# A third pair of k tiles by seven products, and a feed-forward in smaller parts with its down projection between the units

## The chip, the cores and the metric

The kernel runs on one core of one Trainium2 chip. The metric is the time of one execution on the device in microseconds (us), as the median of several runs. The engines of the core work side by side, each through its own list of instructions in order: TensorE (PE) multiplies matrices into PSUM banks, VectorE (DVE) and ScalarE (ACT) do elementwise work, GpSimd (POOL) a little more of that, and SyncE (SP) issues the transfers from memory.

## The reference

The reference is an encoder trunk of two residual layers over 256 tokens of width 2048, all in float32. Layer 0 mixes tokens by grouped-query attention, layer 1 by a gated recurrent block. After either mixer comes the same feed-forward, with its own weights, and that is where the change lies:

```python
def rms_norm(x, g):
    xf = x.astype(jnp.float32)
    y = xf * lax.rsqrt(jnp.mean(xf * xf, axis=-1, keepdims=True) + EPS)
    return (y * g.astype(jnp.float32)).astype(x.dtype)

def swiglu(h, w_gate, w_up, w_down):
    return (jax.nn.silu(h @ w_gate) * (h @ w_up)) @ w_down

# every layer i:
#   x = x + mixer(rms_norm(x, norm_mix[i]))
#   x = x + swiglu(rms_norm(x, norm_ffn[i]), ffn_w_gate[i], ffn_w_up[i], ffn_w_down[i])
```

`w_gate` and `w_up` are 2048 x 5632, `w_down` is 5632 x 2048.

## The kernel before

**Precision.** Every float32 operand is split into a high part (`hi`) and a low part (`lo`), and a product is three matmuls: high x high, low x high, high x low (`product`, lines 253 to 259; L255, L256 and L258 are those three). For weights, a transfer of 512 KB fills a buffer `raw` (128 x 1024), ScalarE casts it to `hi` (L110) and VectorE subtracts to get `lo` (L111). `raw`, `hi` and `lo` have five buffers each, so weights are made a few transfers ahead of their use and no further.

**One feed-forward unit.** The 5632 hidden columns are worked in 11 units of 512 columns (`unit` in `ffn`, lines 670 to 703). The 16 k tiles of the normed activations are taken as 8 pairs `c`. A pair in the plain way takes one transfer of `w_gate` and one of `w_up`, and each meets two k tiles, two halves of the tokens and three matmuls: 24 matmuls of 128x512 per pair. A pair named in `SEVEN` is worked by a 2x2 block scheme with seven products in place of eight (Strassen's in Winograd's form; the blocks are token halves by k tiles on one side and k tiles by gate and up on the other): 21 matmuls. `load_seven` (lines 115 to 139) makes what it needs of the weights: one wide cast (L123) and subtraction (L124), four additions of 128x512 (L126) for the sums `ws`, a narrow cast (L127) and subtraction (L128), and two wide casts (L131) and subtractions (L132) for the high and low parts `wsh`, `wsl` of the sums. The sums have one buffer each. The activations' side of the scheme (`form`, lines 382 to 395) is made once per layer and pair when the norm's input is turned, column group by column group.

The accumulators are PSUM banks of two pools of four. `m1, p5, p7, p6` are taken from one (`bank`, tag `pm`), `c11, c21, c12, c22` from the other (`new_acc`, tag `acc`). When the last pair in `SEVEN` is over, ScalarE copies `m1` (L688) and VectorE combines the first four banks (L689 to L692). At the unit's end VectorE adds `c11` and `c21` (L695), ScalarE applies Silu, VectorE makes the gated product (L698, L699) and turns it in 32x32 blocks (L339), ScalarE sets the blocks in place in sixteen copies (L346), and the result is split into an `act` tile (L701, L702).

**The down projection** runs over four groups of 512 output columns (`wide_project`, two banks each, 12 matmuls per transfer), and each group is added to the residual `x_tm` (`add_residual`, L279).

**Order.** The hidden columns are cut in parts of 16, 16 and 12 tiles of 128, four, four and three units. The kernel runs the units of the first part; then for each part the first unit of the next one, the whole down projection of this part, and the other units of the next. So units follow each other in rows of five, four and two. The last part's down projection (`groups`) runs its first two column groups over all but the last unit's tiles first. TensorE's order is that of the program text. The order on the other engines is set by the framework's planner, which simulates all engines with its own cost figures and sends instructions out as they become ready; on the chip each engine then keeps that order. The order of the weight transfers is written out beforehand (`ffn_order`) and must agree with the program's.

Of the kernel before, what the change touches and what calls it, by code (L numbers as in the profile page):

```python
# [13 lines left out]
F32R = mybir.dt.float32r  # L14
# [4 lines left out]
P = 128  # L19
S = 256  # L20
# [4 lines left out]
GROUP = NQ // NKV  # L25
NBLK = 8
DFF = 5632
PARTS = [16, 16, 12]
UNIT = 4
SEVEN = (0, 4)  # L30
HALF = 8
CHUNK = HALF * P
WIDE = 512
NW = D // WIDE
# [33 lines left out]
def trunk(ctx, tc, w, out):  # L68
    nc = tc.nc
    act, dve, pool, pe, sync = nc.scalar, nc.vector, nc.gpsimd, nc.tensor, nc.sync  # L70
# [3 lines left out]
    xp = ctx.enter_context(tc.tile_pool(name="xp", bufs=16))  # L74
# [7 lines left out]
    def nm(s):  # L82
        uid[0] += 1
        return f"{s}_{uid[0]}"

    def tmp(tag, shape=(P, S), dt=F32, bufs=2):
        pl = tp if tag in COMMON else scope[-1]
        return pl.tile(list(shape), dt, tag=tag, name=nm(tag), bufs=bufs)
# [50 lines left out]
    def halves(src):  # L139
        return [src[:, a : a + HALF, :] for a in range(0, KT, HALF)]  # L140

    def pairs(src):
        return [src[c] for c in range(src.shape[0])]

    def out_order(src, late=1):
        groups = [pairs(src[g]) for g in range(NW)]
        return sum([g[:-late] for g in groups[:2]] + [g[-late:] for g in groups[:2]] + groups[2:], [])

    def ffn_order(l):
        at = np.cumsum([0] + PARTS) // UNIT  # L150
        units = []
        for i in range(at[-1]):
            both = [(w[f"w_gate{l}"][i, c], w[f"w_up{l}"][i, c]) for c in range(KT // 2)]
            units.append(sum(([b] if c in SEVEN else list(b) for c, b in enumerate(both)), []))
        seq = sum(units[: at[1]], [])
        for p in range(len(PARTS)):
            more = units[at[p + 1] : at[p + 2]] if p + 1 < len(PARTS) else []
            down = w[f"w_down{l}_{p}"]
            seq += sum(more[:1], []) + (sum(map(pairs, down), []) if more else out_order(down, UNIT // 2)) + sum(more[1:], [])
        return seq  # L160

    order = [w["w_k"][i] for i in range(2 * KT // 4)]
    order += sum((halves(w["w_qv"][h % 20]) for h in range(NQ, NQ + 20)), [])
# [1 line left out]
    for b in range(-1, NBLK):  # L165
        xin = range(2 * b + 2, 2 * b + 4) if b + 1 < NBLK else []
        yin = range(KT + 2 * b, KT + 2 * b + 2) if b >= 0 else []
        both = [halves(w["w_in"][c]) for c in (*xin, *yin)]
# [4 lines left out]
    def half():  # L173
        n = taken[0]
        taken[0] += 1
        if n == 0:
            return load_half(order[n], 2, partial(load_x, 0, 4))
        if n < KT // 2 and n % 2 == 0:
            load_x(2 * n, 4)
        if n == KT // 2 - 2:  # L180
            load_tables()
        got = (load_seven if isinstance(order[n], tuple) else load_half)(order[n])
        if n == KT // 2 + 1:
            follow(sync.dma_start(out=x_tm, in_=w["xt"]), newest["load"])
        if n in (KT // 2 + 2, KT // 2 + 3):
            token_squares(n - KT // 2 - 2)
        return got
# [22 lines left out]
    def new_acc():  # L210
        return ps_a.tile([P, 2 * S], F32, tag="acc", name=nm("acc"))
# [49 lines left out]
    def wide(accs, xs, k0, total, fresh=None):  # L261
        hi, lo = half()
        fresh = fresh or (k0 == 0, k0 == 0)
        for j in range(CHUNK // WIDE):
            k = k0 + j
            wh, wl = (t[:, j * WIDE : (j + 1) * WIDE] for t in (hi, lo))
            for a in range(2):
                product(accs[a], block(xs, k, a), (wh, wl), j == 0 and fresh[a], k == total - 1)

    def wide_project(xs, total):  # L270
        accs = [new_acc() for _ in range(2)]
        for k0 in range(0, total, 2):
            wide(accs, xs, k0, total)
        return accs

    def add_residual(g, accs, norm, store=False):
        for a in range(2):
            o = x_tm[:, a, g * WIDE : (g + 1) * WIDE]
            dve.tensor_tensor(o, o, accs[a], ALU.add)  # L279
            if store:  # L280
                sync.dma_start(out=out[:, a, g * WIDE : (g + 1) * WIDE], in_=o)
        if norm is not None:
            norm.add(g)

    def groups(xs, total, ready, between, done):
        front = [[new_acc() for _ in range(2)] for _ in range(2)]
        for accs in front:
            for k0 in range(0, ready, 2):
                wide(accs, xs, k0, total)
        between()  # L290
        for g in range(NW):
            for k0 in range(ready, total, 2) if g < 2 else ():
                wide(front[g], xs, k0, total)
            done(g, front[g] if g < 2 else wide_project(xs, total))
# [23 lines left out]
    at = ctx.enter_context(ExitStack())  # L318
# [30 lines left out]
    class Norm:  # L349
# [24 lines left out]
        def turn(self, g):  # L374
# [3 lines left out]
            for i in range(2):  # L378
                if self.g[0] == "norm_ffn" and 2 * g + i in SEVEN:
                    self.form(2 * g + i, t[:, 2 * i : 2 * i + 2, :])  # L380

        def form(self, c, src):
# [4 lines left out]
            for i, x, y, op in (  # L387
# [3 lines left out]
                pool.tensor_tensor(t[:, i, :], x, y, op)  # L391
            hi, lo = (tmp(f"f{n}", (P, 4, P), F32R, bufs=len(SEVEN)) for n in "hl")
            act.copy(hi, t)
# [222 lines left out]
        later(d_sc, scores)  # L616

    def act_four():
        return xp.tile([P, UNIT, 2 * S], F32R, tag="act", name=nm("act"), bufs=5)

    def act_tiles(n):
        return [t[:, i, :] for t in [act_four() for _ in range(n // UNIT)] for i in range(UNIT)]
# [43 lines left out]
    def ffn(norm, nxt):  # L666
        def bank():
            return ps_m.tile([P, 2 * S], F32, tag="pm", name=nm("pm"))

        def unit():  # L670
            xs, r = norm.xs, [norm.r[:, a : a + 1] for a in range(2)]
            m1, p5, p7, p6 = (bank() for _ in range(4))
            c11, c21, c12, c22 = (new_acc() for _ in range(4))
            for c in range(KT // 2):
                if c not in SEVEN:
                    wide((c11, c21), xs, 2 * c, KT, (False, False))
                    wide((c12, c22), xs, 2 * c, KT, (False, c == 1))
                    continue
                wt, first, end = half(), c == SEVEN[0], c == SEVEN[-1]
                n1, n3, n2, n4 = norm.forms[c]  # L680
                a11, a12, a22 = block(xs, 2 * c, 0), block(xs, 2 * c + 1, 0), block(xs, 2 * c + 1, 1)
                for o, x, y in ((m1, a11, "b11"), (p5, n1, "t1"), (p7, n3, "t3"), (p6, n2, "t2")):
                    product(o, x, wt[y], first, end)
                for o, x, y in ((c21, a22, "t4"), (c11, a12, "b21"), (c12, n4, "b22")):
                    product(o, x, wt[y], first, False)
                if end:
                    base, v, u, x = (tmp(f"e{i}", (P, 2 * S), bufs=1) for i in range(4))
                    act.copy(base, m1)  # L688
                    dve.tensor_tensor(u, base, p6, ALU.add)  # L689
                    dve.tensor_tensor(v, u, p5, ALU.subtract)  # L690
                    dve.tensor_tensor(u, u, p7, ALU.add)
                    dve.tensor_tensor(x, u, p5, ALU.subtract)  # L692
            h = tmp("hid", (P, 2, 2 * S), bufs=1)
            for o, y, b in ((base, base, c11), (u, u, c21)):
                dve.tensor_tensor(o, y, b, ALU.add)  # L695
            for a, (o, y, b) in enumerate(((base, v, c12), (u, x, c22))):
                table_act(o, o, AF.Silu, scale=r[a])
                dve.tensor_tensor(h[:, a, :], b, y, ALU.subtract)  # L698
                dve.scalar_tensor_tensor(h[:, a, :], h[:, a, :], r[a], o, ALU.mult, ALU.mult)  # L699
            t, ht = act_four(), turn_blocks(h, (act,), h)  # L700
            act.copy(t[:, :, :S], ht)  # L701
            dve.tensor_tensor(t[:, :, S:], ht, t[:, :, :S].bitcast(F32), ALU.subtract)  # L702
            return [t[:, k, :] for k in range(UNIT)]

        hid = sum((unit() for _ in range(PARTS[0] // UNIT)), [])
        for p in range(len(PARTS)):
            last = p == len(PARTS) - 1
            cur = hid
            hid = [] if last else unit()
            if last:  # L710
                groups(cur, PARTS[p], PARTS[p] - UNIT, lambda: None, partial(add_residual, norm=nxt, store=nxt is None))
            else:
                for g in range(NW):
                    add_residual(g, wide_project(cur, PARTS[p]), None)
                hid += sum((unit() for _ in range(PARTS[p + 1] // UNIT - 1)), [])
        if nxt is not None:
            nxt.finish()
        scope.pop()
        ft.pop().close()


    nr = Norm("norm_mix", KT)
    ffn(nf, nr)


# [101 lines left out]
    units = [(d, j) for j in range(2) for d in range(2)]  # L827
    blk = nxt = None
    for b in range(-1, NBLK):
        blk, nxt = nxt, Block(b + 1) if b + 1 < NBLK else None  # L830
# [102 lines left out]
```

## Time and profile before

| | |
|---|---|
| median of 3 runs | 2021.25 us (2019.75 to 2022.85) |
| the profiled execution | 2023.0 us, of which its span 2021.3 us |
| granted TensorE clock, mean of the span | 0.995 |
| TensorE busy | 1997.4 us, 99% |
| VectorE busy | 1516.7 us, 75% |
| ScalarE busy | 1290.8 us, 64% |
| GpSimd busy | 232.4 us, 11% |

All times of the trace are counted from the span's start. The first feed-forward begins at 279.3 us and ends about 982; the second begins about 1314 and ends with the span. A busy share is an average over stages, so what matters is read from windows cut at a stage's edges. In a row of a timeline stand start, duration, engine, line, operation, output and inputs, and in brackets how long the engine was idle before and what ended that. Matmuls overlap in the pipeline, so their spacing says more than their durations.

### The profile page before, as it was taken

The numbers are of one execution on the slowest core, as the hardware profiler recorded it, in microseconds if no ns is written. First come the engines' busy times: TensorE is split into PE (matmuls) and PEld (weight loads), VectorE is DVE, ScalarE is ACT, GpSimd is POOL, SyncE is SP. The second block draws the span as 40 slices with busy tenths as digits, with TensorE's granted clock in tenths as the row PEclk, the third lists the DMA queues.
The fourth block names the chain that finished last, engine by engine and source line by source line (L and its number), as shares of the span: only waits on it lengthen the run. The fifth ranks groups of instructions, "written<-read, shape, count | busy, mean of one in ns | idle before, by whom it ended". The sixth has DMA issues, their size and how long they took to land.

```text
span 2021.3 us, 27692 instructions
## 1 busy us (share of the span) xinstructions
PE 1997.4 (99%) x9994; PEld 1702.7 (84%) x9994; DVE 1516.7 (75%) x1958; ACT 1290.8 (64%) x1999; POOL 232.4 (11%) x317
## 2 busy tenths in 40 slices
PE   9999999999999999999899999999999999999999
PEld 7888888888888888888799998888888888888887
DVE  7888688886568865686678886888885578856764
ACT  7566576667446664467779996877665457654562
POOL 0464130000000000001333340400000000000000
PEclk9999999999999999999999999999999999999999
DMA  8444565655666656665555555665666655666654
GB/s 315 135 137 131 182 198 193 209 197 179 216 188 198 208 188 208 197 199 188 173 176 178 190 170 179 188 198 187 208 210 196 195 189 189 215 199 195 199 181 155
DMA packets 108569, 386.04 MB, mean 191 GB/s; under 512 B 12176, under 2 KB 12432, under 8 KB 108304
## 3 DMA queue, kind: packets, MB, share of 16 engines
q1 hardware_dynamic: 108288, 384.26, 58.8%
q8 instruction: 78, 1.28, 0.3%
q14 instruction: 59, 0.48, 0.1%
q10 hardware_dynamic: 144, 0.02, 0.0%
HBM read 382.13 MB, written 2.10 MB: 190 GB/s over the span
## 4 chain that ended last, share of the span: by engine, by line
PE 91%; DVE 3%; POOL 2%; issue 1%; DMA 1%; ACT 1%; SPq 0%; POOLq 0%; ACTq 0%; DVEq 0%
PE acc L258 24%; PE acc L256 24%; PE acc L255 24%; PE acc L235 3%; PE acc L236 3%; PE acc L237 3%; PE pm L258 2%; PE pm L256 2%; PE pm L255 2%; PE acc L224 1%; POOL hb L503 1%; DVE lo L111 1%; PE pm L237 1%; PE pm L236 1%; PE pm L235 1%
## 5 line engine op out<-in xcount | busy, mean ns | idle before, releaser
L111 DVE TENSOR_TENSOR lo<-raw,hi 128x1024 fp32r<-128x1024 f32 (+1 forms) x617 | 754.5, 1235 | 374.4 <-ACT hi L110 369.5
L110 ACT CAST hi<-raw 128x1024 fp32r<-128x1024 f32 (+1 forms) x617 | 639.5, 1049 | 538.2 <-PE acc L256 503.7
L255 PE MATMUL acc<-hi,xg 128*128 128x512 f32 x1100 | 428.0, 389 | 0.0
L256 PE MATMUL acc<-hi,xg 128*128 128x512 f32 x1100 | 428.0, 389 | 0.0
L258 PE MATMUL acc<-lo,xg 128*128 128x512 f32 x1100 | 428.0, 389 | 0.0
L255 PE MATMUL acc<-hi,act 128*128 128x512 f32 x960 | 374.0, 390 | 0.0
L258 PE MATMUL acc<-lo,act 128*128 128x512 f32 x960 | 373.7, 389 | 0.0
L256 PE MATMUL acc<-hi,act 128*128 128x512 f32 x960 | 373.6, 389 | 0.0
L255 PEld LDWEIGHTS acc<-hi,xg 128*128 128x128 f32 x1100 | 206.5, 188 | 42.9
L256 PEld LDWEIGHTS acc<-hi,xg 128*128 128x128 f32 x1100 | 206.5, 188 | 42.9
L258 PEld LDWEIGHTS acc<-lo,xg 128*128 128x128 f32 x1100 | 206.5, 188 | 42.8
L256 PEld LDWEIGHTS acc<-hi,act 128*128 128x128 f32 x960 | 180.2, 188 | 37.4
L258 PEld LDWEIGHTS acc<-lo,act 128*128 128x128 f32 x960 | 180.2, 188 | 37.3
L255 PEld LDWEIGHTS acc<-hi,act 128*128 128x128 f32 x960 | 180.2, 188 | 37.1
L346 ACT COPY hid<-turned 32x256 f32<-32x256 f32 x448 | 180.7, 403 | 10.2 <-DVE turned L339 5.1
L346 POOL COPY hid<-turned 32x256 f32<-32x256 f32 x96 | 63.8, 665 | 801.0 <-DVE turned L339 729.7
L235 PE MATMUL acc<-xg,hi 128*128 128x256 f32 x512 | 145.6, 284 | 0.0
L236 PE MATMUL acc<-xg,hi 128*128 128x256 f32 x512 | 145.3, 284 | 0.0
L237 PE MATMUL acc<-xg,lo 128*128 128x256 f32 x512 | 145.0, 283 | 0.0
L224 PE MATMUL acc<-xg,hi 128*128 128x512 f32 x384 | 128.2, 406 | 1.9 <-DVE xg L361 1.9
L131 ACT CAST wsh<-ws 128x1024 fp32r<-128x1024 f32 x88 | 92.2, 1050 | 45.7 <-DVE ws L126 45.7
L132 DVE TENSOR_TENSOR wsl<-ws,wsh 128x1024 fp32r<-128x1024 f32 x88 | 107.7, 1226 | 0.0
(215 smaller groups left out, 2650.3 us busy)
## 6 DMA issues: line engine op xcount, KB each, us to landing
raw<-in_w_gate_dram SPq DMA_DIRECT2D x176, 512.0 KB, 4.1
raw<-in_w_up_dram SPq DMA_DIRECT2D x176, 512.0 KB, 4.0
raw<-in_w_down_dram SPq DMA_DIRECT2D x176, 512.0 KB, 4.3
raw<-in_w_in_dram SPq DMA_DIRECT2D x64, 512.0 KB, 4.4
raw<-in_w_qv_dram SPq DMA_DIRECT2D x40, 512.0 KB, 4.1
raw<-in_w_o_dram SPq DMA_DIRECT2D x32, 512.0 KB, 3.5
raw<-in_w_out_dram SPq DMA_DIRECT2D x32, 512.0 KB, 3.6
graw<-in_w_gates_dram SPq DMA_DIRECT2D x32, 256.0 KB, 3.4
```

The costliest lines, as they stand in the source:

```text
L110: newest["cast"] = act.copy(hi[:, sl], raw[:, sl])
L111: dve.tensor_tensor(lo[:, sl], raw[:, sl], hi[:, sl].bitcast(F32), ALU.subtract)
L131: act.copy(hs[:, sl, :], sums[:, sl, :])
L132: dve.tensor_tensor(ls[:, sl, :], sums[:, sl, :], hs[:, sl, :].bitcast(F32), ALU.subtract)
L224: pe.matmul(acc, w, xs[k], start=(k == 0), stop=stop)
L235: pe.matmul(o, hi, x[:, :S], start=start, stop=False)
L236: pe.matmul(o, hi, x[:, S:], start=False, stop=False)
L237: pe.matmul(o, lo, x[:, :S], start=False, stop=stop)
L255: pe.matmul(o, xh, wh, start=start, stop=False)
L256: pe.matmul(o, xl, wh, start=False, stop=False)
L258: pe.matmul(o, xh, wl, start=False, stop=stop)
L346: (eng.copy if eng is act else eng.tensor_copy)(to[:, :, :, i, :], of[:, :, :, j, :])
```

## The change

A third pair of k tiles, `c = 2`, is worked by seven products. The feed-forward is cut in parts of 8, 8, 8, 8 and 12 tiles. After the two units of the first part, each unit is followed by two column groups of the down projection of the part before, until that part's four groups are done (`ffn_plan`): unit, unit, then unit and two groups eight times, then the last unit, and the last part's down projection as before. These groups take their banks from the pool `pm`, not `acc`. The `act` tiles have four buffers for five.

```diff
-PARTS = [16, 16, 12]
+PARTS = [8, 8, 8, 8, 12]
 UNIT = 4
-SEVEN = (0, 4)
+SEVEN = (0, 2, 4)
@@
+    def ffn_plan():
+        at = np.cumsum([0] + PARTS) // UNIT
+        plan = [("unit", i) for i in range(at[1])]
+        for p in range(len(PARTS) - 1):
+            for n, i in enumerate(range(at[p + 1], at[p + 2])):
+                plan.append(("unit", i))
+                plan += [("down", (p, g)) for g in range(2 * n, min(2 * n + 2, NW))]
+        return plan
+
     def ffn_order(l):
-        at = np.cumsum([0] + PARTS) // UNIT
-        units = []
-        for i in range(at[-1]):
+        seq = []
+        for what, i in ffn_plan():
+            if what == "down":
+                seq += pairs(w[f"w_down{l}_{i[0]}"][i[1]])
+                continue
             both = [(w[f"w_gate{l}"][i, c], w[f"w_up{l}"][i, c]) for c in range(KT // 2)]
-            units.append(sum(([b] if c in SEVEN else list(b) for c, b in enumerate(both)), []))
-        seq = sum(units[: at[1]], [])
-        for p in range(len(PARTS)):
-            more = units[at[p + 1] : at[p + 2]] if p + 1 < len(PARTS) else []
-            down = w[f"w_down{l}_{p}"]
-            seq += sum(more[:1], []) + (sum(map(pairs, down), []) if more else out_order(down, UNIT // 2)) + sum(more[1:], [])
-        return seq
+            seq += sum(([b] if c in SEVEN else list(b) for c, b in enumerate(both)), [])
+        return seq + out_order(w[f"w_down{l}_{len(PARTS) - 1}"], UNIT // 2)
@@
-    def wide_project(xs, total):
-        accs = [new_acc() for _ in range(2)]
+    def wide_project(xs, total, bank=new_acc):
+        accs = [bank() for _ in range(2)]
@@
-        return xp.tile([P, UNIT, 2 * S], F32R, tag="act", name=nm("act"), bufs=5)
+        return xp.tile([P, UNIT, 2 * S], F32R, tag="act", name=nm("act"), bufs=4)
@@
-        hid = sum((unit() for _ in range(PARTS[0] // UNIT)), [])
-        for p in range(len(PARTS)):
-            last = p == len(PARTS) - 1
-            cur = hid
-            hid = [] if last else unit()
-            if last:
-                groups(cur, PARTS[p], PARTS[p] - UNIT, lambda: None, partial(add_residual, norm=nxt, store=nxt is None))
+        hid = [[] for _ in PARTS]
+        ends = np.cumsum(PARTS) // UNIT
+        for what, i in ffn_plan():
+            if what == "unit":
+                hid[int(np.searchsorted(ends, i, "right"))] += unit()
             else:
-                for g in range(NW):
-                    add_residual(g, wide_project(cur, PARTS[p]), None)
-                hid += sum((unit() for _ in range(PARTS[p + 1] // UNIT - 1)), [])
+                add_residual(i[1], wide_project(hid[i[0]], PARTS[i[0]], bank), None)
+        groups(hid[-1], PARTS[-1], PARTS[-1] - UNIT, lambda: None, partial(add_residual, norm=nxt, store=nxt is None))
```

## The prediction

> **What bounds the kernel now.** I read the page first (busy shares, chain), then the waits, then the windows cut at the edges of single feed-forward units, then the timelines of TensorE, VectorE and ScalarE around one such edge. From the page:
>
> ```profile
> span 2021.3 us, 27692 instructions
> PE 1997.4 (99%) x9994; PEld 1702.7 (84%) x9994; DVE 1516.7 (75%) x1958; ACT 1290.8 (64%) x1999; POOL 232.4 (11%) x317
> ```
>
> A 99% busy TensorE could still be a waiting one, so the windows decide; the columns are the stretch, its length, and the busy time and instruction count of each engine. The first two rows hold both feed-forwards, then come one unit in a run of units, the four column groups of one down projection, and the unit behind it:
>
> ```profile
> 240.00:980.00 740.00, 740.00 (x3267) 612.78 (x3266) 555.60 (x608) 460.01 (x652) 37.28 (x56) 1.00 0.61 197
> 1227.00:2015.00 788.00, 788.00 (x3479) 652.58 (x3478) 576.49 (x635) 471.30 (x648) 27.61 (x41) 1.00 0.61 195
> 363.65:405.80 42.15, 42.15 (x187) 34.91 (x186) 35.75 (x41) 28.30 (x40) 0.00 (x0) 1.00 0.60 200
> 490.13:577.16 87.03, 87.03 (x385) 72.07 (x384) 51.36 (x51) 42.34 (x52) 0.00 (x0) 1.00 0.62 193
> 577.16:619.32 42.16, 42.16 (x187) 34.91 (x186) 32.22 (x37) 21.49 (x23) 0.00 (x0) 1.00 0.61 195
> ```
>
> TensorE is not idle for one moment of either feed-forward, at clock 1.00. Its rate comes from the starts of two units that follow each other (first and last row; the other two are used below):
>
> ```profile
> 363.65 0.39 PE L255 MATMUL pm<-hi,xg 128*128 128x512 f32 x1
> 382.01 0.39 PE L255 MATMUL acc<-hi,xg 128*128 128x512 f32 x1
> 577.17 0.39 PE L255 MATMUL pm<-hi,xg 128*128 128x512 f32 x1
> 405.81 0.39 PE L255 MATMUL pm<-hi,xg 128*128 128x512 f32 x1
> ```
>
> A unit has 2x21 + 6x24 = 186 matmuls by the code, so (405.81 - 363.65)/186 = 0.2267 us from one to the next (the 0.39 us are overlapped). The waits show the other engines behind it:
>
> ```profile
> ACT hi L110 <- PE acc L256: 503.7, 301, 3.0
> DVE lo L111 <- ACT hi L110: 369.5, 254, 6.7
> DVE ws L126 <- DMA raw<-in_w_up_dram: 46.6, 25, 4.4
> ```
>
> ScalarE waits for TensorE to give weight buffers back, VectorE for ScalarE. The kernel is bound by TensorE, but a unit leaves VectorE only 42.15 - 35.75 = 6.4 us.
>
> **What the change removes.** A pair of k tiles by seven products has 21 matmuls in place of 24. One more such pair in each of 11 units of 2 layers removes 3x22 = 66 matmuls, and 66 x 0.2267 = **15.0 us**, all on the path that sets the end. The down projections keep their matmuls: the 44 k tiles are only cut differently. For one matmul of this shape the Trainium skill (TensorE: Matmul & The Clock Gate, "Wait — 56ns, not 53.3ns?") gives 215.7 ns with a warm clock, by which the gain would be 14.2 us; the trace has 226.7 ns, and that is used.
>
> **What it adds to VectorE and ScalarE.** Durations overlap a little, so I take distances between starts, from the timeline of VectorE and then of ScalarE behind the unit start at 363.65:
>
> ```profile
> 363.18 1.37 DVE L698 TENSOR_TENSOR hid<-acc,e 128x512 f32<-128x512 f32 x2
> 364.46 1.40 DVE L699 SCALAR_TENSOR_TENSOR hid<-hid,nr,e 128x512 f32<-128x512 f32 x2
> 366.92 1.24 DVE L339 STREAM_TRANSPOSE turned<-hid 128x1024 f32<-128x1024 f32 x1
> 368.83 2.36 DVE L111 TENSOR_TENSOR lo<-raw,hi 128x1024 fp32r<-128x1024 f32 x2 [0.68 <-ACT hi L110]
> 371.11 0.69 DVE L126 TENSOR_TENSOR ws<-raw,raw 128x512 f32<-128x512 f32 x1
> 371.71 0.68 DVE L126 TENSOR_TENSOR ws<-raw 128x512 f32<-128x512 f32 x1
> 377.40 1.23 DVE L111 TENSOR_TENSOR lo<-raw,hi 128x1024 fp32r<-128x1024 f32 x1 [3.67 <-ACT hi L110]
> 378.54 1.22 DVE L132 TENSOR_TENSOR wsl<-ws,wsh 128x1024 fp32r<-128x1024 f32 x1
> ```
> ```profile
> 369.66 6.63 ACT L346 COPY hid<-turned 32x256 f32<-32x256 f32 x16
> 376.31 1.05 ACT L110 CAST hi<-raw 128x1024 fp32r<-128x1024 f32 x1
> 381.07 0.61 ACT L127 CAST hi<-raw 128x512 fp32r<-128x512 f32 x1
> 381.58 2.00 ACT L110 CAST hi<-raw 128x1024 fp32r<-128x1024 f32 x2
> ```
>
> VectorE starts 1024-wide work every 1.14 us (371.11 - 368.83, two) and 512-wide work every 0.60. The plain pair needs two wide subtractions, 2.28 us; the pair by seven needs three wide (L124, two L132) and five narrow (four L126, L128), 3.42 + 3.00 = 6.42. That is **+4.14 us of VectorE per unit**. ScalarE starts a wide cast every 0.96 us (376.31 to the next, and 2.00 for two) and the narrow one in 0.51: three wide and one narrow for two wide, **+1.5 us**. So a unit will hold 35.75 + 4.14 = 39.9 us of VectorE work in 183 x 0.2267 = 41.5 us: 96%, still under TensorE, if nothing idles.
>
> Where a unit is followed by two column groups over 8 tiles, TensorE gets 2x48 = 96 matmuls, 21.8 us, for 8 wide subtractions and 4 residual additions, 8x1.14 + 4x0.68 = 11.8 us of VectorE: together 51.7 in 63.3 us (82%). The new order makes this the rule. What stays without that relief are the first three units of each layer, with **two edges per layer where unit follows unit** (the last part's third unit has groups on both sides). Before, units ran in rows of five, four and two.
>
> **The edge between two units.** There VectorE finishes the old unit (L698 to L339 above, later L702) while TensorE runs the new one's first pairs. The tightest weight in the trace is the second half of pair 3: its subtraction starts at 377.40 and ends 1.23 later, 378.63; TensorE takes it at 382.01. A lead of 3.38 us. After the change 4.14 us more of VectorE work lies in front of it and TensorE comes 3 matmuls, 0.68 us, sooner: 3.38 - 4.14 - 0.68 = **-1.4 us**. From below: the 3.67 us of idle ahead of that row may be filled with the new work, then the lead stays positive and the price is 0. From above: the sixteen copies (L346, 6.63 us, until 376.29) stand ahead of the new cast of weight sums; behind it 0.96 + 1.14 bring its low part to 378.4, while TensorE wants it 48 matmuls into the unit, 363.65 + 10.88 = 374.5: 3.9 us. I take 1.4, nearest the row of the lead, for 4 edges: **+5.8 us**. Behind it the next thing late would be pair 4 by seven products.
>
> **The other edits, at nothing.** The down groups take their two banks from the unit's pool. At each of 16 returns from a group to a unit, the third product wants a bank 6 matmuls (1.36 us) into the unit, the fourth 2.04. The one return in view:
>
> ```profile
> 576.70 1.36 DVE L279 TENSOR_TENSOR x<-x,acc 128x512 f32<-128x512 f32 x2
> ```
>
> The first addition is over by 577.4, the pair at 578.06, 0.9 us after the unit's start at 577.17, so both banks are in time by 1.1 us; with one wide subtraction more in front (1.14) it is a draw, with two about 1.1 us is lost. Lower bound 0, upper 16 x 1.1 = 18 us; I take 0, the row itself. Thirty-two more residual additions (32 x 0.68 = 22 us of VectorE) lie under the groups, where VectorE is busy 51.36 of 87.03 us; uncovered they would cost their 22 us. The third form of the activations:
>
> ```profile
> L385 ACT ACTIVATE fv<-hid,pk 128x256 f32<-128x256 f32 x8 | 3.6, 496 | 0.0
> L391 POOL TENSOR_TENSOR fw<-fv 128x128 f32<-128x128 f32 x8 | 4.6, 600 | 15.6 <-ACT fv L385 15.6
> L391 POOL TENSOR_TENSOR fw<-fw,fv 128x128 f32<-128x128 f32 x4 | 2.0, 493 | 0.3
> L391 POOL TENSOR_TENSOR fw<-fv,fw 128x128 f32<-128x128 f32 x4 | 2.0, 492 | 0.3
> L393 ACT CAST fh<-fw 128x512 fp32r<-128x512 f32 x4 | 2.5, 617 | 2.6 <-POOL fw L391 2.6
> L394 DVE TENSOR_TENSOR fl<-fw,fh 128x512 fp32r<-128x512 f32 x4 | 2.7, 680 | 0.0
> ```
>
> Per layer 2x0.50 + 2x0.60 + 2x0.49 + 0.62 + 0.68 = 4.5 us in a row, for column group 1 of the output projection, two groups ahead of its use (2 x 96 matmuls, 43.5 us): covered; uncovered 9 us in all. Four activation tiles for five: every reader of a tile's predecessor has ended a unit before it is written. The weight loads keep sizes and number and only change places on SP's queue, where down loads now sit between unit loads; they wait there for raw buffers. The adds already waited 46.6 us for 44 second halves; 22 more are 23 us of VectorE idle at that rate, under the 11.6 us per unit that groups leave free, save at the four edges, where it counts among the causes of the 1.4.
>
> **Sum.** The profiled execution took 2023.0 us (span 2021.3 and 1.7 around it): 2023.0 - 15.0 + 5.8 = 2013.8. It was 1.75 above the median of the runs, 2021.25, so the forecast is **2012**.
>
> **Rivals.** *Full gain*: the planner fills the idle 3.67 us and no edge stalls: 2021.25 - 15.0 = 2006.3. For it: TensorE has no gap in either feed-forward, and 96% is under 100%. Against it: VectorE is in order and waited 3.67 us at that very edge.
> *Copies ahead of the sums*: all four edges pay 3.9: 2021.25 - 15.0 + 15.6 = 2021.9, no change. For it: the sixteen copies ran unbroken as soon as the transpose was done, and would again. Against it: with its sums added before 363, the cast goes ahead of them.
> *The first unit too* (the slower side): the same late sums also where the output projection hands over to the first unit. There, before, the sums of the second such pair came at these times:
>
> ```profile
> 287.71 0.68 DVE L126 TENSOR_TENSOR ws<-raw,raw 128x512 f32<-128x512 f32 x1
> 291.86 1.22 DVE L132 TENSOR_TENSOR wsl<-ws,wsh 128x1024 fp32r<-128x1024 f32 x1
> 975.00:1000.00 25.00, 17.82 (x111) 16.36 (x110) 15.13 (x25) 17.65 (x32) 4.81 (x14) 0.88 0.51 165
> ```
>
> Left there, the low part ends at 293.1, wanted 10.88 us into a unit that begins 84.3 us ahead of the one at 363.65, two units of 42.16 us, at 290.2: 2.9 us, twice. 15.6 + 5.8 = 21.4, so 2027.7. It turns slower once an edge and a first unit together cost more than 15 us. Against it: the first unit's adds had slack to move forward. The last row shows that a waiting TensorE also loses clock, 0.88 where it was busy 17.82 of 25 us. The Trainium skill (TensorE: Matmul & The Clock Gate, "What's actually happening") says that about 3.4 us without work halve the clock for at least as long; by that, an estimate, each of the four 3.9 us stalls could cost up to 1.7 us more, 2027.7 + 6.8 = 2034.5. Stalls as short as the forecast's would not set it off.
> *Banks late*: all 16 returns lose 1.1 us: 2021.25 - 15.0 + 18 = 2024, within the noise.
>
> **How the numbers follow.** Forecast 0.41, full gain 0.25, copies 0.18, first unit too 0.12, banks 0.04. About 0.2% (4 us) is what a measurement here tells from no change. Faster: 0.41 + 0.25 = 0.66; same: 0.18 + 0.04 = 0.22; slower 0.12. The range goes from just under the full gain, 2005, over the copies' case to 2022; beyond it lie the slower case and late banks, 0.16. The forecast's own range is 2006 to 2017.
>
> **What would show it.** Matmuls 9994 - 66, at the same 0.2267 us. VectorE near 40 us in each unit; TensorE with gaps only near pairs 2 to 4 of each layer's second and third unit, 1 to 2 us each, released by the low part of weight sums (L132's successor) or by plain low parts; none at returns from groups. Wrong would be: gaps in most units behind groups (banks or VectorE bound everywhere), gaps over 3 us at every edge, or a span longer outside the feed-forwards.

## The result, and the profile after

The changed kernel takes **2034.0 us** (median of 4 runs, 2032.0 to 2035.4) against 2021.2 us before (4 runs): a ratio of 1.0067, 95% interval 1.0055 to 1.0080. It is slower by 13 us, where 2012 and a range of 2005 to 2022 had been forecast. The page of the changed kernel begins:

```profile
span 2032.4 us, 27838 instructions
PE 1992.2 (98%) x9928; PEld 1690.1 (83%) x9928; DVE 1633.3 (80%) x2124; ACT 1324.2 (65%) x2049; POOL 242.4 (12%) x325
```

The 66 matmuls are gone (9994 to 9928). The code below the diff has moved: L255, L256 and L258 are now L261, L262 and L264, the residual addition L279 is L285, the copies L346 are L352. The windows of the changed kernel show, in this order, the first feed-forward, the second, and one unit with its two column groups:

```profile
275.90:986.06 710.16, 699.84 (x3071) 575.03 (x3069) 581.74 (x655) 443.44 (x617) 22.35 (x32) 1.00 0.61 196
1318.73:2028.56 709.83, 701.19 (x3070) 576.04 (x3068) 570.55 (x637) 424.26 (x566) 8.24 (x8) 1.00 0.59 193
426.93:491.25 64.32, 63.55 (x281) 52.32 (x280) 52.47 (x59) 38.13 (x51) 0.00 (x0) 1.00 0.61 197
```

Before, each feed-forward had 11 x 186 + 1056 = 3102 matmuls and took 3102 x 0.2267 = 703.1 us without a gap. Now each has 3069, which would take 695.6, and takes 710: **TensorE loses 14 us per layer that it never lost before**, 28.7 us in all, against 15.0 us saved. VectorE is not full: 52.47 of 64.32 us in a unit with its groups, where the prediction had 51.7. The waits of TensorE say where the time went; each wait stands twice, for the matmul and, a little longer, for its weight load:

```profile
PEld pm L261 <- DVE x L285: 20.0, 16, 2.6
PE pm L261 <- DVE x L285: 13.2, 16, 2.2
PEld pm L264 <- DVE wsl L132: 6.8, 6, 1.8
PE pm L264 <- DVE wsl L132: 4.3, 6, 1.4
```

The first is new, and there are exactly sixteen of it: one at each return from a pair of column groups to a unit. TensorE's timeline at one return, cut to each product's first matmul and the row behind the wait (the unit starts at 426.93):

```profile
426.93 0.39 PE L261 MATMUL pm<-hi,xg 128*128 128x512 f32 x1
...
427.61 0.39 PE L261 MATMUL pm<-wsh,fh 128*128 128x512 f32 x1
...
428.29 0.39 PE L261 MATMUL pm<-wsh,fh 128*128 128x512 f32 x1
...
428.74 0.39 PE L264 MATMUL pm<-wsl,fh 128*128 128x512 f32 x1
429.90 0.50 PE L261 MATMUL pm<-wsh,fh 128*128 128x512 f32 x1 [0.77 <-DVE x L285]
430.24 0.39 PE L262 MATMUL pm<-wsh,fl 128*128 128x512 f32 x1
```

The fourth product, due at 428.97, starts at 429.90, and the matmul behind it comes 0.11 us late as well. VectorE at the same time:

```profile
427.14 0.68 DVE L285 TENSOR_TENSOR x<-x,pm 128x512 f32<-128x512 f32 x1
427.95 0.69 DVE L126 TENSOR_TENSOR ws<-raw,raw 128x512 f32<-128x512 f32 x1
428.56 0.68 DVE L126 TENSOR_TENSOR ws<-raw 128x512 f32<-128x512 f32 x1
429.17 0.68 DVE L285 TENSOR_TENSOR x<-x,pm 128x512 f32<-128x512 f32 x1
```

The two residual additions of the last group, side by side at 576.70 before, now have two additions of weight sums for pair 2 between them. So the group's second bank is given back at 429.85, 2.9 us into the unit and not 0.9, and the fourth product waits for it. From the distances between matmul starts, the sum over each one's excess above 0.2267 us: the 16 returns cost 17.6 us, the first units and the unit-to-unit edges 10.4 us; the 0.7 us left over is spread thin. VectorE's order is the same at all sixteen returns. Fifteen cost about 1.0 us each; the sixteenth costs 2.4, because there the first of the two additions also waits 1.5 us for a transfer.

### The profile page after: what moved, and what is told of

Same layout as the page of the kernel before. It is cut to its first block, busy times and chain, and to the rows that moved or that the text cites. A ratio compares the mean times of both kernels' runs of the same rounds, so it can differ in the third digit from the quotient of the medians.

```text
span 2032.4 us, 27838 instructions
## 1 busy us (share of the span) xinstructions
PE 1992.2 (98%) x9928; PEld 1690.1 (83%) x9928; DVE 1633.3 (80%) x2124; ACT 1324.2 (65%) x2049; POOL 242.4 (12%) x325
## 4 chain that ended last, share of the span: by engine, by line
PE 76%; DVE 13%; DMA 3%; issue 3%; ACT 2%; POOL 2%; DVEq 0%; SPq 0%; POOLq 0%; ACTq 0%
PE acc L261 15%; PE acc L262 15%; PE acc L264 15%; PE pm L261 6%; PE pm L264 6%; PE pm L262 5%; DVE lo L111 4%; PE acc L241 3%; PE acc L242 3%; PE acc L243 3%; DMA raw<-in_w_up_dram 2%; DVE ws L126 2%; DVE wsl L132 2%; PE acc L230 1%; POOL hb L509 1%
## 5 line engine op out<-in xcount | busy, mean ns | idle before, releaser
L111 DVE TENSOR_TENSOR lo<-raw,hi 128x1024 fp32r<-128x1024 f32 (+1 forms) x573 | 703.5, 1235 | 237.1 <-ACT hi L110 226.8
L261 PE MATMUL acc<-hi,xg 128*128 128x512 f32 x946 | 368.3, 389 | 0.0
L262 PE MATMUL acc<-hi,xg 128*128 128x512 f32 x946 | 368.3, 389 | 0.0
L264 PE MATMUL acc<-lo,xg 128*128 128x512 f32 x946 | 368.3, 389 | 0.0
L261 PEld LDWEIGHTS acc<-hi,xg 128*128 128x128 f32 x946 | 177.8, 188 | 37.1
L264 PEld LDWEIGHTS acc<-lo,xg 128*128 128x128 f32 x946 | 177.7, 188 | 37.0
L262 PEld LDWEIGHTS acc<-hi,xg 128*128 128x128 f32 x946 | 177.7, 188 | 36.9
L131 ACT CAST wsh<-ws 128x1024 fp32r<-128x1024 f32 x132 | 136.6, 1049 | 109.0 <-PE acc L262 94.1
L261 PE MATMUL pm<-hi,act 128*128 128x512 f32 x512 | 199.2, 389 | 0.0
L262 PE MATMUL pm<-hi,act 128*128 128x512 f32 x512 | 199.2, 389 | 0.0
L264 PE MATMUL pm<-lo,act 128*128 128x512 f32 x512 | 199.2, 389 | 0.0
L352 ACT COPY hid<-turned 32x256 f32<-32x256 f32 x448 | 180.8, 404 | 23.2 <-DVE turned L345 18.1
L132 DVE TENSOR_TENSOR wsl<-ws,wsh 128x1024 fp32r<-128x1024 f32 x132 | 159.5, 1221 | 26.1 <-ACT wsh L131 26.0
L261 PE MATMUL acc<-hi,act 128*128 128x512 f32 x448 | 174.7, 390 | 0.0
L264 PE MATMUL acc<-lo,act 128*128 128x512 f32 x448 | 174.4, 389 | 0.0
L262 PE MATMUL acc<-hi,act 128*128 128x512 f32 x448 | 174.3, 389 | 0.0
L352 POOL COPY hid<-turned 32x256 f32<-32x256 f32 x96 | 67.3, 701 | 790.5 <-DVE turned L345 719.1
```

What stands on the lines that cost most here:

```text
L111: dve.tensor_tensor(lo[:, sl], raw[:, sl], hi[:, sl].bitcast(F32), ALU.subtract)
L131: act.copy(hs[:, sl, :], sums[:, sl, :])
L132: dve.tensor_tensor(ls[:, sl, :], sums[:, sl, :], hs[:, sl, :].bitcast(F32), ALU.subtract)
L261: pe.matmul(o, xh, wh, start=start, stop=False)
L262: pe.matmul(o, xl, wh, start=False, stop=False)
L264: pe.matmul(o, xh, wl, start=False, stop=stop)
```

## The experiments

Two readings stood against each other. *Late bank*: the returns cost what they cost because of the place of one residual addition and of the bank it holds. *VectorE full*: it is too busy behind a return, and the bank is only where that shows. Each run below was timed against the kernel before on the same chip, and its ratio is to that.

### Other banks, same order on VectorE

```diff
-                add_residual(i[1], wide_project(hid[i[0]], PARTS[i[0]], bank), None)
+                add_residual(i[1], wide_project(hid[i[0]], PARTS[i[0]]), None)
```

> The changed kernel with one edit taken back: the down groups between the units take their two banks from the pool of c11 to c22 (tag acc), as before, not from that of m1 to p6 (tag pm). VectorE's written order, with two additions of weight sums between the two residual additions of the last group ahead of a unit, stays. Late-bank theory: the 16 returns from a group to a unit cost 16 x 1.05 = 17 us because the fourth product waits for the second residual addition; the acc banks are wanted only 18 matmuls (4.1 us) into the unit or later, so the waits vanish: 2034.0 - 17 = 2017, the waits at the unit-to-unit edges (about 10 us) stay. Rival, VectorE full: it is too busy behind every return and the bank is only where that shows; the waits come back at the weight sums of pairs 2 and 4: 2030 or more.

2015.7 us (2012.7 to 2020.3), ratio 0.9977 (0.9966 to 0.9988). The waits on L285 at returns are gone, with the two additions of sums still between the residual additions in VectorE's list. The feed-forwards:

```profile
277.07:978.55 701.48, 698.71 (x3071) 576.76 (x3069) 581.11 (x655) 444.21 (x617) 22.33 (x32) 1.00 0.62 198
1311.77:2011.61 699.84, 697.04 (x3070) 575.45 (x3068) 569.62 (x637) 424.66 (x566) 8.23 (x8) 1.00 0.61 196
```

They are 18.7 us shorter than with the change as it was made, while VectorE's work is the same within 2 us: what was taken away is a wait, not work. With this one word taken back, the change is faster than the kernel before.

### Same banks, other order on VectorE

```diff
-        dve.tensor_tensor(lo[0], raw[0], hi[0][:].bitcast(F32), ALU.subtract)
+        first = dve.tensor_tensor(lo[0], raw[0], hi[0][:].bitcast(F32), ALU.subtract)
+        held = [first]
         for o, x, y in ((t1, b11, b12), (t3, b12, b22), (t2, t1, b22), (t4, t2, b21)):
-            dve.tensor_tensor(o, x, y, ALU.add)
+            held.append(dve.tensor_tensor(o, x, y, ALU.add))
+        if newest.get("pair") == SEVEN[1] and "residual" in newest:
+            for i in held:
+                follow(i, newest["residual"])
+            del newest["residual"]
```

(Not shown are two lines that keep the last residual addition in `newest["residual"]` and the pair that the unit is about to load in `newest["pair"]`.)

> The changed kernel with its banks, and only an order on VectorE added: the subtraction and the additions of weight sums for pair 2 of a unit come behind the last residual addition ahead of that unit, so that nothing stands between the two residual additions. Late-bank theory: the second addition ends about 1.5 us after the unit's start at the latest, the fourth product wants the bank at 2.04 us, so the 16 waits vanish as with other banks: 2017. Rival, VectorE full: pair 2 is only made later, 2030 or more. Rival, the shared pool itself is too small: a wait of a part of 1.05 us stays at each return, 2022 to 2034.

2017.9 us (2016.6 to 2019.5), ratio 0.9983 (0.9974 to 0.9992). No return waits. The two additions are side by side again, in one row of VectorE's timeline (L290 is the residual addition here):

```profile
429.03 1.28 DVE L290 TENSOR_TENSOR x<-x,pm 128x512 f32<-128x512 f32 x2
```

The unit there starts at 428.81, so both banks are back 1.5 us into it. Two edits that share nothing but the bank's return, each with about the forecast gain: the late-bank reading holds, and neither VectorE's load nor the pool by itself explains the 17 us. This run's edges and first units cost 12.9 us in place of 10.4: in a layer's first unit the edit also holds pair 2 back, behind the residual additions of the mixer's output, and the first units lose 3.6 and 4.5 us where they lost 0.5.

### The late product later, same banks and same order on VectorE

```diff
-                for o, x, y in ((m1, a11, "b11"), (p5, n1, "t1"), (p7, n3, "t3"), (p6, n2, "t2")):
-                    product(o, x, wt[y], first, end)
-                for o, x, y in ((c21, a22, "t4"), (c11, a12, "b21"), (c12, n4, "b22")):
-                    product(o, x, wt[y], first, False)
+                for o, x, y in ((m1, a11, "b11"), (p5, n1, "t1"), (p7, n3, "t3"), (c21, a22, "t4"),
+                                (c11, a12, "b21"), (p6, n2, "t2"), (c12, n4, "b22")):
+                    product(o, x, wt[y], first, end and o in (m1, p5, p7, p6))
```

> The changed kernel (2034 us), its banks and VectorE's order with the two additions of weight sums between the residual additions kept; only TensorE's order in a pair by seven products changes: the fourth product into a pm bank (p6) comes behind the products into c21 and c11, so that the bank released last is wanted 15 matmuls (3.4 us) into a unit, not 9 (2.04 us). The second residual addition ends about 2.9 us into the unit. Late-bank theory: 0.95 us of wait against 1.36 us won, the 16 waits go, 2017; what stays are the edges. Rival, VectorE full behind returns, or the weight sums late: TensorE waits elsewhere in the pair, 2030 or more.

2014.8 us (2013.9 to 2017.5), ratio 0.9973 (0.9962 to 0.9984). The unit here starts at 425.37. VectorE's second residual addition still comes behind the two sums, and TensorE's first matmul of the late product, in the second fence, no longer minds:

```profile
425.59 0.68 DVE L285 TENSOR_TENSOR x<-x,pm 128x512 f32<-128x512 f32 x1
...
427.50 0.68 DVE L285 TENSOR_TENSOR x<-x,pm 128x512 f32<-128x512 f32 x1
```
```profile
428.77 0.39 PE L261 MATMUL pm<-wsh,fh 128*128 128x512 f32 x1
```

The bank is back at 428.18, 2.8 us into the unit as before; it is wanted at 3.4, not 2.0. Fifteen of the sixteen waits are gone. One is left, of 1.6 us by the matmul starts: there the first addition of sums waited 2.0 us for its transfer, and the bank came back 4.8 us into the unit.

```profile
PE pm L261 <- DVE x L285: 1.3, 1, 1.3
```

A fourth run in this group tells nothing:

```diff
-            m1, p5, p7, p6 = (bank() for _ in range(4))
+            m1, p5, p6, p7 = (bank() for _ in range(4))
```

> The changed kernel (2034 us) with one edit: the banks of the third and the fourth product are taken in the other order, so that the bank released last by the groups is wanted 6 matmuls into the unit, not 9; VectorE's order there is the same. Late-bank theory: each of the 16 waits grows by 3 matmuls, 0.68 us: 2034 + 11 = 2045. Rival, the wait is for VectorE as a whole or for the weight sums: no change, 2034.

2034.3 us, ratio 1.0069 (1.0052 to 1.0086): no change, and TensorE's wait still stands ahead of the fourth product. Its premise was wrong: which bank a product gets is not fixed by the line that names the four. The wait stayed with the product that opens its bank last, so the edit changed nothing that counts and does not speak against the reading that the three others bear out.

### Each half of the change alone

The plan without the third pair:

```diff
-SEVEN = (0, 2, 4)
+SEVEN = (0, 4)
```

> The changed kernel with two pairs by seven products, as before, in the new order of units and groups and with the new banks. Late-bank theory: without the third pair VectorE has no weight sums to add at that moment and the planner leaves the two residual additions together, so there is no wait at the 16 returns, nor at the edges: 2021, the time before. Rival, the shared pool itself: the returns cost their 17 us with two pairs as well, 2038. Rival, VectorE full: 2021 too.

2020.2 us (2018.5 to 2021.4), ratio 0.9997 (0.9988 to 1.0007), and no gap at all in the feed-forwards, with the pm banks under the groups. With two pairs the new order and the shared pool cost nothing. At the return whose unit starts at 425.06, VectorE has the two additions together:

```profile
425.28 1.28 DVE L285 TENSOR_TENSOR x<-x,pm 128x512 f32<-128x512 f32 x2
```

They are over 1.5 us into the unit, as at the other fifteen returns of this run, against 0.9 at 576.70 in the kernel before: the new order alone brings the bank back 0.6 us later, and still in time. The third pair in the old order (the kernel before, with):

```diff
-PARTS = [16, 16, 12]
+PARTS = [12, 12, 12, 8]
-SEVEN = (0, 4)
+SEVEN = (0, 2, 4)
-        return xp.tile([P, UNIT, 2 * S], F32R, tag="act", name=nm("act"), bufs=5)
+        return xp.tile([P, UNIT, 2 * S], F32R, tag="act", name=nm("act"), bufs=4)
```

> The kernel before with three pairs by seven products, in the old order (the first unit of a part, the whole down projection of the part ahead, the other units) and with the old banks; the parts are 12, 12, 12 and 8 tiles for the room of the third form, so units follow units at 7 edges per layer. Late-bank theory with edges of their own: no wait at returns; in the changed kernel the two edges of a layer cost 2.9 and 1.3 us and the first unit 0.5; at 1.3 to 2.9 us for 14 edges this gives 2021 - 15 + 1 + 18 to 41 = 2025 to 2048. Rival, the third pair is free wherever banks are not late: 2007.

2047.8 us (2045.4 to 2051.4), ratio 1.0134 (1.0118 to 1.0150): the slow end of what was expected, though its edges are not.

```profile
PE pm L258 <- DVE wsl L132: 13.8, 22, 1.4
PE acc L255 <- ACT act L701: 6.3, 2, 3.1
```

The 14 edges cost 22 us (1.2 to 2.4 each, from the distances between matmul starts), all at the third pair by seven products, near the lower end of the 18 to 41 us expected. The second row is a cost of this run's own that the expectation left out: with a last part of 8 tiles the last unit's `act` comes too late for the last projection. With the matmuls at a lower clock behind it (0.68 granted from 952.3 to 957.7 us) it takes 12.8 us in the two layers. So the interleaving earns its place: without it the third pair costs 22 us at edges and saves 15.

### What the edges cost, and why

With the other banks (2015.7 us) some 10 us are still lost, nearly all in pair 4 of each layer's second and third unit. (The 0.5 us of each first unit is another late bank, in the other pool: there `c12` waits for a residual addition behind the mixer, `PE acc L261 <- DVE x L285: 0.5, 2, 0.3`.) In the changed kernel ScalarE's timeline, and below it VectorE's, show the second unit (it starts at 317.9 us):

```profile
329.43 6.64 ACT L352 COPY hid<-turned 32x256 f32<-32x256 f32 x16 [2.42 <-DVE turned L345]
336.09 1.05 ACT L123 CAST hi<-raw 128x1024 fp32r<-128x1024 f32 x1
...
340.42 1.04 ACT L131 CAST wsh<-ws 128x1024 fp32r<-128x1024 f32 x1
```
```profile
337.18 1.23 DVE L124 TENSOR_TENSOR lo<-raw,hi 128x1024 fp32r<-128x1024 f32 x1 [2.40 <-ACT hi L123]
...
342.33 1.22 DVE L132 TENSOR_TENSOR wsl<-ws,wsh 128x1024 fp32r<-128x1024 f32 x1
```

The sixteen copies of the unit before stand ahead of the casts for pair 4; VectorE is idle for 2.40 us behind them, and the last part of the sums is ready at 343.5. Whether the copies or VectorE's 96% are to blame was put to three runs, each on top of the other banks. Of their diffs only the lines that matter are shown.

The copies shared with GpSimd:

```diff
-            t, ht = act_four(), turn_blocks(h, (act,), h)
+            t, ht = act_four(), turn_blocks(h, (act, pool), h)
```

> The kernel of the run with the groups in the other banks (2015.7 us), and in a unit the sixteen block copies shared between ScalarE and GpSimd, eight each, so that ScalarE holds 3.3 us of them in place of 6.6. There TensorE still waits at the third pair by seven products of each layer's second unit (2.3 us) and third unit (1.3 us), and 0.5 us in the first. Copies theory: that pair's casts come 3.3 us sooner, so these waits, 2 x 3.6 = 7.3 us, go: 2008 to 2010. Rival, VectorE full at the edges (96%): the waits stay or grow, as VectorE slows beside GpSimd: 2015 or more.

2008.3 us (2006.5 to 2009.4), ratio 0.9940 (0.9924 to 0.9957). From 10 us the edges and first units come down to 1.9 us.

```profile
327.75 3.32 ACT L352 COPY hid<-turned 32x256 f32<-32x256 f32 x8 [2.41 <-DVE turned L345]
331.09 1.06 ACT L123 CAST hi<-raw 128x1024 fp32r<-128x1024 f32 x1
```

The unit starts 1.6 us earlier in this run (316.4), the cast for pair 4 5.0 us earlier: it comes 3.4 us sooner in the unit, about what ScalarE was spared. VectorE has the same work there, and some of it even goes slower beside GpSimd's copies (last section), so its load is not what the waits came from.

Other places for the three pairs:

```diff
-SEVEN = (0, 2, 4)
+SEVEN = (0, 3, 5)
```

> The kernel with the groups in the other banks (2015.7 us), and pairs 0, 3 and 5 by seven products in place of 0, 2 and 4; the work on every engine is the same, only its place in the unit changes, the second such pair 24 matmuls (5.4 us) later. Copies theory: the sixteen copies of the unit before are over before the casts of the last of these pairs are due, and the waits of 7.3 us go: 2008. Rival, VectorE full: 96% stays 96%, the waits move to another pair and stay about as long: 2013 to 2017.

2034.0 us (2033.4 to 2035.7), ratio 1.0067 (1.0052 to 1.0082): 26 us off the copies reading's number, and worse than its rival's too. ScalarE and VectorE at the edge, now with pair 3 behind it:

```profile
335.03 6.63 ACT L352 COPY hid<-turned 32x256 f32<-32x256 f32 x16 [2.94 <-DVE turned L345]
341.68 1.04 ACT L131 CAST wsh<-ws 128x1024 fp32r<-128x1024 f32 x1
```
```profile
342.75 1.23 DVE L132 TENSOR_TENSOR wsl<-ws,wsh 128x1024 fp32r<-128x1024 f32 x1 [5.45 <-ACT wsh L131]
```

The copies do not end at a fixed time that one could plan around; they end 6.63 us behind the transpose, and here they stand between the two casts of pair 3's sums. VectorE idles 5.45 us, and each layer loses 12 to 13 us at its two edges. The cause in these rows is the one that the reading named; its number was wrong, because it took the transpose to stay where it was. With pairs 0, 2 and 4 in the run with the other banks it starts 9.7 us into this unit (328.75, the unit at 319.08), here 13.2 (333.75, the unit at 320.59). Why it comes later stays open.

No third pair behind an edge (`SEVEN` of the second and third unit `(0, 4)`, of the others `(0, 2, 4)`):

```diff
+def sevens(i):
+    return (0, 4) if i in (1, 2) else SEVEN
```

> The kernel with the groups in the other banks (2015.7 us), and in the second and third unit of each layer, those that follow a unit, only pairs 0 and 4 by seven products. That is 12 matmuls more (2.7 us). If the waits at edges come from the third pair there, in whichever way, they go, 7.3 us: 2015.7 + 2.7 - 7.3 = 2011. If they come from the order of units and groups itself: 2018.

2009.9 us (2008.3 to 2010.2), ratio 0.9945 (0.9930 to 0.9960), with no gap left but 0.5 us in each layer's first unit. The waits at edges come from the third pair there; this run does not tell the copies from VectorE's load.

### More pairs where there is room

The unit and the order of the transfers take their pairs from `sevens(i)`, as in the run above, and the groups keep the other banks; both are left out of the diff:

```diff
-SEVEN = (0, 2, 4)
+SEVEN = (0, 2, 4, 6)
+def sevens(i):
+    return (0, 4) if i < 3 else SEVEN
```

> The kernel with the groups in the other banks; the first three units of each layer with pairs 0 and 4 by seven products, the other eight with pairs 0, 2, 4 and 6. Against the kernel before, 2 x 8 x 2 x 3 = 96 matmuls less, 21.8 us, and no edge with more than two pairs. If VectorE's load counts over a unit with its two groups (35.75 + 2 x 4.14 + 11.8 = 55.8 of 62.6 us, 89%), nothing stalls: 2020.3 - 21.8 = 1998.5, to 2002 with short waits. Rival, pairs by seven products with one plain pair between them are too dense whatever follows: each of the 16 such units waits 1.3 to 2.3 us as at the edges, 2019 to 2035.

**2000.1 us** (1997.3 to 2000.6), ratio 0.9895 (0.9881 to 0.9910): the best version of all, 20.6 us ahead of the kernel before beside it and 34 ahead of the change as it was made. The first feed-forward, and one unit with its groups:

```profile
275.31:967.55 692.24, 692.24 (x3055) 573.39 (x3054) 596.41 (x687) 451.24 (x630) 21.81 (x36) 1.00 0.62 201
443.69:506.30 62.61, 62.61 (x278) 51.83 (x277) 55.85 (x65) 39.50 (x52) 0.00 (x0) 1.00 0.62 201
```

VectorE works 55.85 of 62.61 us, as the sum from the rows of before had it (55.8), and TensorE waits for nothing there; in the second feed-forward 0.9 us are lost. A unit with its groups can hold four such pairs at 89% of VectorE. A unit alone holds three, at 96%, only where the copies do not stand in front: with them shared, 1.9 us were lost.

Two attempts to go on failed. First, three pairs in the first three units and shared copies on top of that, with

```diff
+    return (0, 2, 4) if i < 3 else SEVEN
```

> The run with four pairs behind groups (2000.1 us) with the first three units of each layer at pairs 0, 2 and 4 by seven products and the block copies of a unit shared between ScalarE and GpSimd. 18 matmuls less, 4.1 us: 1996, if GpSimd's slowing of VectorE (512-wide work 0.80 us apart beside it, 0.60 alone) finds room under the groups, as VectorE's 89% there says. Rival, VectorE full in the denser units: 1998 to 2010.

2005.0 us (2003.4 to 2009.6), ratio 0.9928 (0.9913 to 0.9942): faster than before, slower than the version it was built on. Nearly 5 us per layer are lost in the first three units (in the second layer 1.6 of them to a lower clock behind the wait), at the bank of `c12` and at pair 4's sums, though the first three units are written as in the run with shared copies alone, where they lost 0.6 and 1.2 us. Which step of the order there costs the 4 us is open.

Then four pairs everywhere, with `SEVEN` for every unit and the shared copies kept:

> The same with pairs 0, 2, 4 and 6 in every unit. Another 18 matmuls less, 4.1 us, but in the first three units VectorE has 35.75 + 2 x 4.14 = 44.0 us of work, and some more beside GpSimd, against 180 x 0.2267 = 40.8 of TensorE. If a unit without groups is bound by VectorE, each of the two units behind an edge loses about 3 to 5 us per layer, 12 to 20 in all: 2004 to 2012, slower than with three pairs there. If the weights made ahead carry it over: 1992.

2021.1 us (2019.6 to 2022.5), ratio 1.0004 (0.9995 to 1.0014). It has 132 matmuls less than the kernel before, 29.9 us, and loses 29.8 us, all but 0.7 of them in the first three units. Some 7 us of that are matmuls at half clock behind the longest waits (0.50 granted from 324.7 to 330.2 us); the waits themselves are led by these:

```profile
PE pm L267 <- DVE e L705: 7.6, 2, 3.8
PE pm L270 <- DVE wsl L138: 5.8, 4, 2.6
```

(L705 is the last combination of the pm banks, L138 the low part of the sums.) There a unit without groups has, by the sum in the expectation, more work for VectorE than for TensorE (44.0 against 40.8 us), and a last pair at 6 puts the combination of the four pm banks just ahead of the next unit that wants them.

## Why the prediction was wrong

**What the change removes** was right: 66 matmuls, at the same 0.2267 us, 15.0 us. So was VectorE's load, 51.7 us forecast and 52.47 measured for a unit with its groups, and so was the new order at nothing: with two pairs, shared banks included, it changed the time by 0.1 us of 2020. VectorE's waits for second halves did not grow by 23 us, as supposed, but fell from 46.6 to 25.6 us; no term of the sum hung on them.

**The step that failed** is the one on the banks, "Lower bound 0, upper 16 x 1.1 = 18 us; I take 0, the row itself." It measured 17.6 us. The row was one return in a kernel in which the next pair by seven products began 93 matmuls into the unit; with the third pair it begins 45 in, its sums fall due at the very moment of the return, and VectorE's written order put two of them between the residual additions. The slack of 1.1 us went in two steps. The first addition starts 0.2 us behind the unit's start and no longer 0.5 ahead of it; the new order does that with two pairs as well, and alone it costs no wait. The two narrow additions in between, in some returns with a short wait for a transfer, put the second residual addition 1.4 us further back, and with that the bank is 0.9 us late. The text held the condition, only for the wrong place ("with one wide subtraction more in front (1.14) it is a draw, with two about 1.1 us is lost"): it asked how long the queue ahead of the first addition was, and not what could come between the two. That the upper bound of 18 us, worked out from that queue, comes so near is luck.

**The edges** were mis-sized: 5.8 us for the four, 9.4 measured in the changed kernel, 1.3 us at each layer's third unit, 2.9 and 3.8 at its second; the 3.8 has about 1.6 us of lower clock in it (last section). The first units, put at nothing, cost 1.0 more, which makes the 10.4. The lead was worked out at pair 3 and the copies' price at pair 2, and the waits came at pair 4, which the text had named as the next thing late. The cause was the one named in the rival *Copies ahead of the sums*, priced there at 3.9 per edge; halving the copies took most of it away.

**The rivals and the range.** *Banks late* had 0.04 and, with no price for the edges, 2024; it happened, and the edges with it: 2021.2 - 15.0 + 17.6 + 10.4 = 2034.2. The range ended at the copies' price alone; banks and edges, which do not exclude each other, were never added. *The first unit too*, the rival on the slower side, did add two costs and lay outside the range. Its 2034.5, with the estimate for the clock on top, meets the measured time by luck: first units lost 0.5 us each, not 2.9, and the returns were at nothing in it.

**What would show it** did its work: "gaps in most units behind groups (banks or VectorE bound everywhere)" was named as the sign that the forecast is wrong.

## What to carry to other kernels

Where a change makes two stages share a pool of banks, find for each hand-over the instruction that gives the last bank back and ask what the planner may put in front of it and between its parts; a single hand-over seen in the old trace did not hold once new work fell due at that moment. An engine that is under 100% over a unit can still hold up the others inside it: what counts is the longest run of in-order work (here 6.6 us of copies) ahead of the next thing that somebody waits for. And when two costs are bounded separately, the range needs their sum.

## What the runs showed of the hardware

**The clock can fall after a wait far shorter than the prediction had supposed.** In the changed kernel, at the edge of the second layer, TensorE waited twice within one product:

```profile
1383.64 0.50 PE L261 MATMUL pm<-wsh,fh 128*128 128x512 f32 x1 [0.28 <-ACT wsh L131]
1383.97 0.40 PE L262 MATMUL pm<-wsh,fl 128*128 128x512 f32 x1
1385.72 0.68 PE L264 MATMUL pm<-wsl,fh 128*128 128x512 f32 x1 [1.36 <-DVE wsl L132]
...
1386.63 0.63 PE L262 MATMUL acc<-wsh,xg 128*128 128x512 f32 x1
1387.06 0.63 PE L264 MATMUL acc<-wsl,xg 128*128 128x512 f32 x1
```
```profile
1384.00:1389.50 5.50, 4.14 (x12) 2.96 (x11) 5.23 (x6) 2.88 (x4) 0.00 (x0) 0.69 0.71 224
```

Matmuls then start 0.43 us apart until 1389.2, and the window's granted clock is 0.69; this cost about 1.6 us more. Idle gaps of 0.28 and 1.36 us were enough. The Trainium skill (TensorE: Matmul & The Clock Gate, "What's actually happening") has the clock halved after an idle window of about 3.4 us, from which the prediction concluded that stalls of 1 to 2 us would not set it off. The measurement decides: such gaps can. They need not: nearly the same gaps at the same edge of the first layer (0.48 and 1.35 us) left the clock alone. In the run with the other banks it was the other way round: the first layer's edge lost its clock (0.39 and 1.36 us; 0.69 granted from 342.6 to 348.1 us), the second's kept it (0.41 and 1.36 us; 1.00). What decides between the two was not tried.

**GpSimd's copies slow VectorE beside them.** In the run with shared copies, eight on GpSimd took 7.90 us, and VectorE's narrow additions came 0.80 us apart in place of 0.60:

```profile
327.87 7.90 POOL L352 COPY hid<-turned 32x256 f32<-32x256 f32 x8 [36.98 <-DVE turned L345]
```
```profile
329.55 0.88 DVE L126 TENSOR_TENSOR ws<-raw,raw 128x512 f32<-128x512 f32 x1
330.35 0.88 DVE L126 TENSOR_TENSOR ws<-raw 128x512 f32<-128x512 f32 x1
```

By the Trainium skill (GPSIMD Engine Reference, "1. Specifications") the two engines share their way to SBUF and contend when a VectorE instruction has two inputs from there, as these have; the rows agree. Behind GpSimd's copies, over at 335.8, the next narrow step takes 0.60 us again (336.77 to 337.37).
